# Moving three operands of a seven-product projection ahead of its last producer, and splitting the other four at its end

## The chip, the cores and the metric

The kernel runs on one core of a Trainium2 chip. The metric is device time in microseconds (us) of one execution. Five engines matter: TensorE (PE) multiplies, with its weight loads listed apart (PEld); VectorE (DVE), ScalarE (ACT) and GpSimd (POOL) do the element-wise work; SyncE (SP) issues nearly all DMAs. Each engine works through its own queue in order.

## The reference, cut to what matters

Two decoder layers on a sequence of 1024 with a model width of 1024. Each ends with an output projection, a residual add, an RMSNorm and a convolutional FFN:

```python
def conv_ffn(h, w_up, w_dw, b_dw, w_down):
    u = h @ w_up                                  # 1024 -> 2 * 2816
    u = causal_dwconv(u, w_dw, b_dw)              # width 3
    gate, val = jnp.split(u, 2, axis=-1)
    return (jax.nn.silu(gate) * val) @ w_down

x = x + jnp.concatenate([mix, mem_o], axis=-1) @ w_out[l]
x = x + conv_ffn(rmsnorm(x, g_ffn[l]), w_up[l], w_dw_f[l], b_dw_f[l], w_down[l])
```

Everything is float32 and has to come out with float32 accuracy.

## The kernel before

**Layout.** The residual stream lies transposed in eight tiles `x[0]` to `x[7]` of 128 channels by 1024 tokens; the halves of the sequence are `h0` and `h1` (512 tokens each). A float32 product is made of three matmuls: each operand is split into a rounded high half (a cast on ACT) and the remainder as a low half (a subtraction on DVE or POOL), and high by high, high by low and low by high are added (`split`, L76; `split_gain`, L162, which also applies the norm's gain).

**The up projection** is `h @ w_up` of both FFNs. It is cut into 2 by 2 blocks: the weights of one chunk of 128 gate and 128 value channels into A11, A12 (gate, first and second half of the model width) and A21, A22 (value); the stream into B11 = x[0..3] at h0, B12 at h1, B21 = x[4..7] at h0 and B22 at h1. Instead of eight block products it uses seven, with sums S1 to S4 of the A blocks (on POOL, `sums`, L452) and T1 to T4 of the B blocks (on DVE, `ffn_operands`, L362: L401 makes T1, L405 T2, L407 T3, L409 T4, in place in the tiles of x):

- p1 = A11 B11 and p2 = A12 B21 add up in PSUM bank X,
- p5 = S1 T1 and p3 = S4 B22 in bank V,
- p6 = S2 T2, p7 = S3 T3 and p4 = A22 T4 in bank Y,

and between the products of a bank DVE reads the bank (into `fuv` and `fug`, the two result halves). One product is a chain of 12 matmuls (four tiles k by three matmuls, `chain`, L336, matmuls at L345) of 128x128 weights and 512 columns. There are 22 chunks; the operands of B and T are made once for all of them and stay in SBUF, 56 tiles of 128x512: 24 under the tag `h2` in a pool of their own (`up0`, `up1`, opened by `ffn_begin` before the output projection) and 32 under the tag `h`, which until then hold the output projection's own inputs (`mxh`, `mxl`). Before the change T1, T2 and T3 are the ones in `h2`, and B11, B21, B22 and T4 go into `h`.

**The entry into the FFN.** The output projection adds its results to x tile by tile (`out_part`, L328, the add at L334); the last tile is x[7] both times. `ffn_operands` follows for k = 0 to 3: squares of x[k] and x[k+4] for the norm (ACT, summed by POOL at L396), stores of both to DRAM (SP, L390), then for this k the split or sum of all seven operands. The first two chunks are worked together, as p1, p5, p2, p3, then the norm's statistics (`rstd_rows`, eight tiny matmuls L133 and a row broadcast L123 for each half of the sequence), then p6, p7, p4. From chunk 2 on the loop is p1, p4 of the chunk before, p6, p5, p2, p7, p3.

**What sets the order.** A scheduler orders each engine's queue from the program's order as priority and its own idea of time; a buffer that is reused makes its new writer wait for the last reader of the old tile. The queues below were read from the built programs.

Of the kernel before, what the change touches and what calls it, by code (L numbers as in the profile page):

```python
# [51 lines left out]
class Trunk:  # L52
# [308 lines left out]
    def ffn_operands(self, l):  # L361

        nc = self.nc
        K2 = KD // 2
        gain = f"g_ffn{l}"
        x = self.x
        h0, h1 = slice(0, HS), slice(HS, S)  # L370
        names = ("B11", "B21", "B22", "T1", "T2", "T3", "T4")
        ops = {n: ([None] * K2, [None] * K2) for n in names}
        for n in names:
            for k in range(K2):
                for i in range(2):
                    if n in ("T1", "T2", "T3"):
                        t = self.fp.tile([P, HS], F32R, tag="h2", name=f"f{n}{i}{k}", bufs=6 * K2)
                    else:
                        t = self.htile(f"f{n}{i}{k}")
                    ops[n][i][k] = t  # L380

        def op(n, k):
            return ops[n][0][k], ops[n][1][k]

        acc = self.main.tile([P, S], F32, tag="rb", name="sacc")
        v = nc.vector
        for k in range(K2):
            for q in (k, k + K2):
                for sl in (h0, h1):
                    nc.sync.dma_start(self.d_x[:, q, sl], x[q][:, sl])  # L390
                    if q == 0:
                        nc.scalar.activation(acc[:, sl], x[q][:, sl], AF.Square)
                    else:
                        sq = self.nt("sq")
                        nc.scalar.activation(sq, x[q][:, sl], AF.Square)
                        nc.gpsimd.tensor_tensor(acc[:, sl], acc[:, sl], sq, op=ALU.add)  # L396
            g, g2 = self.vec(gain, k), self.vec(gain, k + K2)
            x11, x12, x21, x22 = x[k][:, h0], x[k][:, h1], x[k + K2][:, h0], x[k + K2][:, h1]
            self.split_gain(*op("B11", k), x11, g)
            nc.scalar.activation(x11, x11, AF.Copy, scale=g)  # L400
            v.scalar_tensor_tensor(x12, x12, g, x11, op0=ALU.mult, op1=ALU.subtract)  # L401
            self.split(*op("T1", k), x12, lo_eng=v)
            self.split_gain(*op("B21", k), x21, g2)
            self.split_gain(*op("B22", k), x22, g2)
            v.scalar_tensor_tensor(x22, x22, g2, x12, op0=ALU.mult, op1=ALU.subtract)  # L405
            self.split(*op("T2", k), x22, lo_eng=v)
            v.tensor_tensor(x11, x22, x11, op=ALU.subtract)  # L407
            self.split(*op("T3", k), x11, lo_eng=v)
            v.scalar_tensor_tensor(x21, x21, g2, x22, op0=ALU.mult, op1=ALU.subtract)  # L409
            self.split(*op("T4", k), x21, lo_eng=v)  # L410
        return ops, acc

    def ffn(self, l):
        nc, tc = self.nc, self.tc
# [2 lines left out]
        def unit(nm):  # L417
            return self.main.tile([P, S], F32, tag="x", name=f"f{nm}")

        with self.fstack:  # L420
# [31 lines left out]
            def sums(c):  # L452

                a, b = raws[c]
                s12 = unit("s12").rearrange("p (k c) -> p k c", k=KD)
                s4 = self.nt("s4").rearrange("p (k c) -> p k c", k=K2)
                g = nc.gpsimd
                g.tensor_tensor(s12[:, lo4], b[:, lo4], b[:, hi4], op=ALU.add)
                g.tensor_tensor(s12[:, hi4], s12[:, lo4], a[:, lo4], op=ALU.subtract)
                g.tensor_tensor(b[:, lo4], a[:, lo4], b[:, lo4], op=ALU.subtract)  # L460
                g.tensor_tensor(s4, a[:, hi4], s12[:, hi4], op=ALU.subtract)
                st[c] = {"A": {"S1": s12[:, lo4], "S2": s12[:, hi4], "S3": b[:, lo4], "S4": s4,
                               "A11": a[:, lo4], "A12": a[:, hi4], "A22": b[:, hi4]}}

# [3 lines left out]

            load(0)
            load(1)
            ops, acc = self.ffn_operands(l)
            sums(0)
            sums(1)
            ybanks = self.ps.tile([P, 2, HS], F32, tag="b2b", name="uY")
            rb = self.main.tile([P, S], F32, tag="rb", name="rb")
            h0, h1 = slice(0, HS), slice(HS, S)
# [16 lines left out]
            def p1(c):  # L495
                d = st[c]
                d["v"] = unit("uv")
                d["g"] = unit("ug")
                d, X = p(c, 1, "A11", "B11", "X", True)
                nc.scalar.copy(d["v"][:, h0], X)  # L500

            def p6(c):
                d, Y = p(c, 6, "S2", "T2", "Y", True)
                nc.vector.tensor_tensor(d["g"][:, h1], Y, d["v"][:, h0], op=ALU.add)
# [4 lines left out]

            def p2(c):  # L510
                d, X = p(c, 2, "A12", "B21", "X", False)
                if c < 2:
                    return
                nc.vector.tensor_tensor(d["g"][:, h0], X, rb[:, h0], op=ALU.mult)
                if c + 1 < NF:
                    sums(c + 1)
                    load(c + 2)

            def late2(c):
# [8 lines left out]
            def p3(c):  # L528
                d, V = p(c, 3, "S4", "B22", "V", False)
                if c > 1:  # L530
                    late3(c)

            def late3(c):
# [30 lines left out]
                return y  # L564


            for f in (p1, p5, p2, p3):
                f(0)
                f(1)
                if f == p2:  # L570
                    rstd_rows()
                    late2(0)
                    late2(1)
            p6(0)
            late3(0)
            p6(1)
            late3(1)
            load(2)
            sums(2)
            load(3)  # L580
            p7(0)
            p7(1)
            p4(0)
            for c in range(2, NF):
                for f, i in ((p1, 0), (p4, -1), (p6, 0), (p5, 0), (p2, 0), (p7, 0), (p3, 0)):
# [92 lines left out]
    def layer_a(self):  # L678
# [270 lines left out]
                self.split(*mx(hf, CT + ct), outs[ct][:, hf * HS:(hf + 1) * HS])  # L949

        wm = [self.load_wm(0, u) for u in range(2)]
        for k in range(KD):
            self.x[k] = self.main.tile([P, S], F32, tag="x", name=f"x1{k}")
            nc.sync.dma_start(self.x[k], self.xT[:, k])

# [46 lines left out]
    def layer_b(self):  # L1002
# [298 lines left out]
            nc.sync.dma_start(self.x[k], self.d_x[:, k])  # L1301

        def out_loads():
            wos[0] = self.load_wo(1, 0)
            for k in (6, 7, 0):
                load_mix(k)
            for k in range(EARLY):
                load_x(k)
            for k in (1, 2, 3):
                load_mix(k)  # L1310
            for m in range(1, EARLY):
                wos[m] = self.load_wo(1, m)

        def out_steps():
            ks = [6, 7, 0, 1, 2, 3]
            d = {}

            def step(m, hf, j):
                k = ks[j]
                sl = slice(hf * HS, (hf + 1) * HS)  # L1320
                wh, wl = wos[m]
                if j == 0:
                    d["u"] = self.ps.tile([P, HS], F32, tag="c0", name="op")
# [3 lines left out]
            return [lambda m=m, hf=hf, j=j: step(m, hf, j) for m in range(EARLY) for hf in range(2)  # L1327
                    for j in range(len(ks))]

        for n, (t, e, I) in enumerate(its):  # L1330
# [21 lines left out]
        self.drain_fill()  # L1352
        stack.close()
        self.ffn_begin(1)
        ms = [m for m in (2, 4, 5, 6, 3, 7)]
        self.ps.n = 0
        for k in ms:
            load_x(k)
# [1 line left out]
        for m in ms:  # L1360
            w = self.load_wo(1, m)
            for hf in range(2):
                self.out_part(m, hf, w, mxh, mxl, order)
            if m == EARLY:
                for m0 in range(EARLY):
                    for hf in range(2):
                        self.out_part(m0, hf, wos[m0], mxh, mxl, order[-2:])

    NRAW = 2
    EARLY = 2  # L1370
    OLOAD = 40
    OFILL = 40
    VMARKS = (1.1, 1.0, 1.1, 0.7, 0)
# [163 lines left out]
```

## Time and profile before

| what | value |
|---|---|
| time, median of 3 runs (lowest, highest) | 2375.9 us (2375.04, 2375.92) |
| the profiled execution's own time, and its span | 2374.32 us, 2372.5 us |
| mean granted clock of TensorE | 0.981 |
| PE busy (share of the span), instructions | 2269.8 us (96%), 10970 |
| DVE busy | 1457.4 us (61%), 1967 |
| ACT busy | 1075.7 us (45%), 1864 |
| POOL busy | 1374.7 us (58%), 1031 |

The span runs from the first to the last instruction. A granted clock of 1.00 is 2.4 GHz, 0.50 is 1.2 GHz. The matmuls of the first FFN's up projection begin at 425.14 us and those of the second's at 1651.16 us; the stretch that begins at each of these points is called the first and the second entry.

### The profile page before, as it was taken

The numbers are of one execution on the slowest core, as the hardware profiler recorded it, in microseconds if no ns is written. First come the engines' busy times: TensorE is split into PE (matmuls) and PEld (weight loads), VectorE is DVE, ScalarE is ACT, GpSimd is POOL, SyncE is SP. The second block draws the span as 40 slices with busy tenths as digits, with TensorE's granted clock in tenths as the row PEclk, the third lists the DMA queues.
The fourth block names the chain that finished last, engine by engine and source line by source line (L and its number), as shares of the span: only waits on it lengthen the run. The fifth ranks groups of instructions, "written<-read, shape, count | busy, mean of one in ns | idle before, by whom it ended". The sixth has DMA issues, their size and how long they took to land.

```text
span 2372.5 us, 29724 instructions
## 1 busy us (share of the span) xinstructions
PE 2269.8 (96%) x10970; PEld 1872.0 (79%) x10970; DVE 1457.4 (61%) x1967; ACT 1075.7 (45%) x1864; POOL 1374.7 (58%) x1031
## 2 busy tenths in 40 slices
PE   6999889899999999999998999999799999999998
PEld 6777678677878887888897888777577787888887
DVE  7479775866666653225646777854766666655225
ACT  6786654533434343223543656844433443443212
POOL 3685946676777765553324444526576868676532
PEclk8999989999999999999999999999899999999999
DMA  6101113122222235333322222342122222235322
GB/s 238 36 27 36 47 45 126 50 89 72 80 80 89 80 112 188 100 107 116 116 86 76 79 74 75 109 148 85 36 89 80 89 71 90 71 129 176 113 71 72
DMA packets 85281, 216.74 MB, mean 91 GB/s; under 512 B 9008, under 2 KB 29232, under 8 KB 85136
## 3 DMA queue, kind: packets, MB, share of 16 engines
q1 hardware_dynamic: 84992, 214.52, 28.2%
q8 instruction: 86, 1.41, 0.2%
q14 instruction: 59, 0.48, 0.1%
q10 hardware_dynamic: 144, 0.32, 0.0%
HBM read 156.94 MB, written 51.58 MB: 88 GB/s over the span
## 4 chain that ended last, share of the span: by engine, by line
PE 44%; DVE 4%; issue 1%; ACT 1%; POOL 1%; DMA 0%; DVEq 0%; ACTq 0%; POOLq 0%; SPq 0%
PE uY L345 7%; PE uV L345 5%; PE uX L345 5%; PE dn L109 3%; PE dn L108 3%; PE dn L110 3%; PE vps L1079 3%; PE pq L108 2%; PE pq L110 2%; PE pq L109 2%; PE op L109 1%; PE op L108 1%; PE fo L1262 1%; PE fo L1261 1%; PE op L110 1%
## 5 line engine op out<-in xcount | busy, mean ns | idle before, releaser
L345 PE MATMUL uY<-fT,fwh 128*128 128x512 f32 x1056 | 333.0, 396 | 9.6 <-DVE fuv L525 6.6
L109 PE MATMUL dn<-gl,wd_hi 128*128 128x512 f32 (+1 forms) x752 | 284.6, 379 | 0.4 <-POOL gl L82 0.4
L108 PE MATMUL dn<-gh,wd_hi 128*128 128x512 f32 (+1 forms) x752 | 280.8, 378 | 1.3 <-ACT fx L618 1.3
L110 PE MATMUL dn<-gh,wd_lo 128*128 128x512 f32 (+1 forms) x752 | 279.1, 375 | 0.0
L619 DVE TENSOR_TENSOR fx<-fx,dn 128x512 f32<-128x512 f32 (+1 forms) x176 | 111.0, 637 | 270.9 <-PE dn L110 269.4
L345 PEld LDWEIGHTS uY<-fT,fwh 128*128 128x128 f32 x1056 | 197.0, 188 | 61.6 <-DVE fuv L525 13.4
L345 PE MATMUL uX<-fB,fwh 128*128 128x512 f32 x704 | 224.1, 398 | 16.8 <-ACT fB L168 7.3
L345 PE MATMUL uY<-fT,fwl 128*128 128x512 f32 x528 | 207.9, 394 | 0.0
L82 POOL TENSOR_TENSOR fwl<-wa,fwh 128x512 fp32r<-128x512 f32 x88 | 118.5, 1347 | 120.1 <-ACT fwh L81 116.6
L82 POOL TENSOR_TENSOR wd_lo<-wd_raw,wd_hi 128x1024 fp32r<-128x1024 f32 x44 | 107.7, 2454 | 128.1 <-ACT wd_hi L81 128.1
L345 PEld LDWEIGHTS uX<-fB,fwh 128*128 128x128 f32 x704 | 132.8, 190 | 50.4 <-ACT fB L168 7.7
L108 PEld LDWEIGHTS dn<-gh,wd_hi 128*128 128x128 f32 x752 | 141.1, 188 | 30.0 <-ACT fx L618 1.7
L110 PEld LDWEIGHTS dn<-gh,wd_lo 128*128 128x128 f32 x752 | 141.1, 188 | 27.2
L109 PEld LDWEIGHTS dn<-gl,wd_hi 128*128 128x128 f32 x752 | 141.3, 188 | 25.8 <-POOL gl L82 0.9
L82 POOL TENSOR_TENSOR fwl<-wb,fwh 128x512 fp32r<-128x512 f32 x88 | 117.2, 1335 | 72.7 <-ACT fwh L81 72.7
L832 POOL TENSOR_TENSOR yp<-yp,ct 128x512 f32<-128x512 f32 x100 | 135.6, 1359 | 27.5 <-ACT ct L831 22.5
L82 POOL TENSOR_TENSOR gl<-g,gh 128x512 fp32r<-128x512 f32 x88 | 116.8, 1348 | 55.1 <-ACT gh L81 55.1
L82 POOL TENSOR_TENSOR fwl<-fs,fwh 128x512 fp32r<-128x512 f32 x88 | 117.9, 1341 | 47.3 <-ACT fwh L81 47.3
L345 PE MATMUL uX<-fB,fwl 128*128 128x512 f32 x352 | 137.8, 394 | 0.0
L81 ACT CAST fwh<-wa 128x512 fp32r<-128x512 f32 x88 | 54.3, 619 | 149.1 <-PE uY L345 105.5
L345 PE MATMUL uV<-fT,fwh 128*128 128x512 f32 x352 | 113.7, 403 | 5.1 <-ACT fT L81 4.3
L345 PEld LDWEIGHTS uY<-fT,fwl 128*128 128x128 f32 x528 | 99.4, 188 | 23.3
(392 smaller groups left out, 6269.9 us busy)
## 6 DMA issues: line engine op xcount, KB each, us to landing
wb<-in_wup SPq DMA_DIRECT2D x44, 512.0 KB
wa<-in_wup SPq DMA_DIRECT2D x44, 512.0 KB
d_g<-fsg SPq DMA_DIRECT2D x44, 512.0 KB
wd_raw<-in_wdn SPq DMA_DIRECT2D x44, 512.0 KB
g<-d_g SPq DMA_DIRECT2D x44, 512.0 KB
d_x<-x SPq DMA_DIRECT2D x32, 256.0 KB
nxs<-d_x SPq DMA_DIRECT2D x32, 256.0 KB
wia_raw<-in_wia SPq DMA_DIRECT2D x14, 512.0 KB
```

What stands on the lines that cost most here:

```text
L81: nc.scalar.copy(hi, src)
L82: (lo_eng or nc.gpsimd).tensor_tensor(lo, src, hi.bitcast(F32), op=ALU.subtract)
L108: nc.tensor.matmul(out, lhsT=ah, rhs=bh, start=start and i == 0, stop=False)
L109: nc.tensor.matmul(out, lhsT=ah, rhs=bl, start=False, stop=False)
L110: nc.tensor.matmul(out, lhsT=al, rhs=bh, start=False, stop=stop and i == n - 1)
L345: mm = nc.tensor.matmul(out, lhsT=w[:, k], rhs=h[k], start=start and k == 0 and j == 0, stop=k == n - 1 and j == 2, skip_group_check=True)
L619: return nc.vector.tensor_tensor(self.x[m][:, sl], self.x[m][:, sl], ps, op=ALU.add)
L832: nc.gpsimd.tensor_tensor(y[:, hf], y[:, hf], c, op=ALU.add)
L1079: nc.tensor.matmul(ps, lhsT=a[hf][k][:, tsl], rhs=w[:, k % 4], start=k == 0 and j == 0, stop=k == KD - 1 and j == 2)
L1261: nc.tensor.matmul(po, lhsT=vs[:, j], rhs=ph[:, u], start=j == 0, stop=False)
L1262: nc.tensor.matmul(po, lhsT=vs[:, j], rhs=pl[:, u], start=False, stop=j == 2 * I + 1)
```

## The change

It changes which operands are made when. B11, T1 and B22 now live in `h2`, the pool that is open during the output projection, and are split there as soon as their tile of x is complete. B21 stays unsplit in x[4..7], and T2, T3 and T4 are kept as plain sums in the tiles of x (T2 over B22, T3 over B11, T4 over T1). They are split into `h` tiles by the new function `late`, called after p1 of the first two chunks. The sum S1 of these two chunks gets small tiles of its own (`sum1`); S2 and S4 share a unit that waits for a tile of x. The order of the products of the first two chunks becomes p1, p5, p3, p2, p6, p7, p4, with the norm's statistics after p6 in the program. In the first layer x[4..7] are loaded ahead of x[0..3]; in the second the output projection works on x[4], x[5] early and x[6], 0, 1, 2, 3, 7 after it, where it was 0, 1 early and then 2, 4, 5, 6, 3, 7. No operation is added or dropped; both programs make the same splits, sums, adds and matmuls.

```diff
-        names = ("B11", "B21", "B22", "T1", "T2", "T3", "T4")
+        names = ("B11", "T1", "B22", "B21", "T2", "T3", "T4")
         ops = {n: ([None] * K2, [None] * K2) for n in names}
-        for n in names:
+        for n in names[:3]:
             for k in range(K2):
                 for i in range(2):
-                    if n in ("T1", "T2", "T3"):
-                        t = self.fp.tile([P, HS], F32R, tag="h2", name=f"f{n}{i}{k}", bufs=6 * K2)
-                    else:
-                        t = self.htile(f"f{n}{i}{k}")
-                    ops[n][i][k] = t
+                    ops[n][i][k] = self.fp.tile([P, HS], F32R, tag="h2", name=f"f{n}{i}{k}", bufs=6 * K2)
...
-            self.split_gain(*op("B11", k), x11, g)
             nc.scalar.activation(x11, x11, AF.Copy, scale=g)
+            self.split(*op("B11", k), x11, lo_eng=v)
             v.scalar_tensor_tensor(x12, x12, g, x11, op0=ALU.mult, op1=ALU.subtract)
             self.split(*op("T1", k), x12, lo_eng=v)
-            self.split_gain(*op("B21", k), x21, g2)
             self.split_gain(*op("B22", k), x22, g2)
             v.scalar_tensor_tensor(x22, x22, g2, x12, op0=ALU.mult, op1=ALU.subtract)
-            self.split(*op("T2", k), x22, lo_eng=v)
             v.tensor_tensor(x11, x22, x11, op=ALU.subtract)
-            self.split(*op("T3", k), x11, lo_eng=v)
-            v.scalar_tensor_tensor(x21, x21, g2, x22, op0=ALU.mult, op1=ALU.subtract)
-            self.split(*op("T4", k), x21, lo_eng=v)
-        return ops, acc
+            v.scalar_tensor_tensor(x12, x21, g2, x22, op0=ALU.mult, op1=ALU.subtract)
+        def late():
+            for k in range(K2):
+                for n, sl, q in (("B21", h0, k + K2), ("T2", h1, k + K2)):
+                    for i in range(2):
+                        ops[n][i][k] = self.htile(f"f{n}{i}{k}")
+                    self.split_gain(*op(n, k), x[q][:, sl], self.vec(gain, q) if n == "B21" else None)
+            for k in range(K2):
+                for n, sl in (("T3", h0), ("T4", h1)):
+                    for i in range(2):
+                        ops[n][i][k] = self.htile(f"f{n}{i}{k}")
+                    self.split(*op(n, k), x[k][:, sl], lo_eng=v)
+        return ops, acc, late
...
             def sums(c):
                 a, b = raws[c]
-                s12 = unit("s12").rearrange("p (k c) -> p k c", k=KD)
-                s4 = self.nt("s4").rearrange("p (k c) -> p k c", k=K2)
+                if c < 2:
+                    s1 = first[c]
+                    u = unit("s24").rearrange("p (k c) -> p k c", k=KD)
+                    s2, s4 = u[:, lo4], u[:, hi4]
+                else:
...
+            def sum1(c):
+                s1 = first[c] = self.nt("s1").rearrange("p (k c) -> p k c", k=K2)
+                b = raws[c][1]
+                nc.gpsimd.tensor_tensor(s1, b[:, lo4], b[:, hi4], op=ALU.add)
...
-            ops, acc = self.ffn_operands(l)
-            sums(0)
-            sums(1)
+            ops, acc, late = self.ffn_operands(l)
...
-            for f in (p1, p5, p2, p3):
-                f(0)
-                f(1)
-                if f == p2:
+            for c in range(2):
+                begin(c)
+                sum1(c)
+            p1(0)
+            p1(1)
+            late()
+            for c in range(2):
+                sums(c)
+            for c in range(2):
+                st[c]["g"] = unit("ug")
+            for f in (p5, p3, p2, p6, p7):
+                for c in range(2):
+                    f(c)
+                if f == p6:
                     rstd_rows()
-                    late2(0)
-                    late2(1)
-            p6(0)
-            late3(0)
-            p6(1)
-            late3(1)
-            load(2)
-            sums(2)
-            load(3)
-            p7(0)
-            p7(1)
+                    for c in range(2):
+                        out2(c)
+                        out3(c)
+                if f == p6:
+                    load(2)
+                    begin(2)
+                    sums(2)
+                    load(3)
             p4(0)
...
-        for k in range(KD):
+        for k in (4, 5, 6, 7, 0, 1, 2, 3):
             self.x[k] = self.main.tile([P, S], F32, tag="x", name=f"x1{k}")
...
-        ms = [m for m in (2, 4, 5, 6, 3, 7)]
+        ms = (6, 0, 1, 2, 3, 7)
...
-    EARLY = 2
+    EARLY = (4, 5)
```

How the change moves instructions is seen at two places, both at the second entry.

DVE there, before. In the names `fT113` is the low half (1) of T1 for tile 3, `x27` is x[7] of the second layer, `L508` is the first add that reads bank V after p5. The last operands of k = 2, then of k = 3:

```order
L82 TENSOR_TENSOR fT112_14373<-x22_13948,fT102_14372 128x512
L82 TENSOR_TENSOR fT212_14381<-x26_13954,fT202_14380 128x512
L82 TENSOR_TENSOR fT312_14389<-x22_13948,fT302_14388 128x512
L82 TENSOR_TENSOR fT412_14397<-x26_13954,fT402_14396 128x512
L169 SCALAR_TENSOR_TENSOR fB1113_14351<-x23_13956,vecs_63,fB1103_14350 128x512
L169 SCALAR_TENSOR_TENSOR fB2113_14359<-x27_13958,vecs_63,fB2103_14358 128x512
L142 RECIPROCAL rs_14668<-sd_14666 128x4
L169 SCALAR_TENSOR_TENSOR fB2213_14367<-x27_13958,vecs_63,fB2203_14366 128x512
L401 SCALAR_TENSOR_TENSOR x23_13956<-x23_13956,vecs_63 128x512
L405 SCALAR_TENSOR_TENSOR x27_13958<-x27_13958,vecs_63,x23_13956 128x512
L82 TENSOR_TENSOR fT113_14375<-x23_13956,fT103_14374 128x512
L407 TENSOR_TENSOR x23_13956<-x27_13958,x23_13956 128x512
```

DVE at the same place, now; the last output tile's add, B22 for k = 3 (`fB2213`), the three sums and T2's low half for k = 3 stand directly ahead of these rows, and `L530` is the same add as `L508`:

```order
L82 TENSOR_TENSOR fT310_14548<-x20_13950,fT300_14547 128x512
L82 TENSOR_TENSOR fT410_14552<-x20_13950,fT400_14551 128x512
L142 RECIPROCAL rs_14722<-sd_14720 128x4
L82 TENSOR_TENSOR fT311_14556<-x21_13952,fT301_14555 128x512
L82 TENSOR_TENSOR fT411_14560<-x21_13952,fT401_14559 128x512
L142 RECIPROCAL rs_14730<-sd_14728 128x4
L82 TENSOR_TENSOR fT312_14564<-x22_13954,fT302_14563 128x512
L82 TENSOR_TENSOR fT412_14568<-x22_13954,fT402_14567 128x512
L82 TENSOR_TENSOR fT313_14572<-x23_13956,fT303_14571 128x512
L530 TENSOR_TENSOR fuv_14479<-uV_14589,fuv_14479 128x512
L82 TENSOR_TENSOR fT413_14576<-x23_13956,fT403_14575 128x512
L530 TENSOR_TENSOR fuv_14498<-uV_14607,fuv_14498 128x512
```

T1's low half for k = 3 (`fT113`) stood seven rows behind T4's for k = 2 (`fT412`) and behind the splits of `x27`; now it stands ahead of the last tile's add. T3 and T4, whose splits stood with their own k, now follow all together, ahead of the adds that read bank V.

POOL there, before, from the last square but one (`sacc`) on, `fs12` being the unit with S1 and S2, `wb` with S3, `ns4` with S4:

```order
L396 TENSOR_TENSOR sacc_14400<-sacc_14400,nsq_14511 128x512
L458 TENSOR_TENSOR fs12_14537<-wb_13944 128x512
L458 TENSOR_TENSOR fs12_14543<-wb_13946 128x512
L459 TENSOR_TENSOR fs12_14537<-fs12_14537,wa_14340 128x512
L460 TENSOR_TENSOR wb_13944<-wa_14340,wb_13944 128x512
L459 TENSOR_TENSOR fs12_14543<-fs12_14543,wa_14342 128x512
L460 TENSOR_TENSOR wb_13946<-wa_14342,wb_13946 128x512
L82 TENSOR_TENSOR fwl_14591<-fs12_14537,fwh_14590 128x512
L82 TENSOR_TENSOR fwl_14624<-wa_14340,fwh_14623 128x512
L461 TENSOR_TENSOR ns4_14538<-wa_14340,fs12_14537 128x512
```

POOL there, now, `ns1` being S1 and `fs24` the unit with S2 and S4:

```order
L392 TENSOR_TENSOR sacc_14368<-sacc_14368,nsq_14455 128x512
L484 TENSOR_TENSOR ns1_14475<-wb_13944 128x512
L484 TENSOR_TENSOR ns1_14477<-wb_13946 128x512
L392 TENSOR_TENSOR sacc_14368<-sacc_14368,nsq_14459 128x512
L473 TENSOR_TENSOR wb_13944<-wa_14340,wb_13944 128x512
L82 TENSOR_TENSOR fwl_14591<-ns1_14475,fwh_14590 128x512
L473 TENSOR_TENSOR wb_13946<-wa_14342,wb_13946 128x512
L82 TENSOR_TENSOR fwl_14591<-ns1_14477,fwh_14590 128x512
L471 TENSOR_TENSOR fs24_14579<-ns1_14475,wa_14340 128x512
L471 TENSOR_TENSOR fs24_14583<-ns1_14477,wa_14342 128x512
L472 TENSOR_TENSOR fs24_14579<-wa_14340,fs24_14579 128x512
L82 TENSOR_TENSOR fwl2_14684<-fs24_14579,fwh2_14683 128x512
```

S1 of both chunks now comes first, and the last square's sum goes ahead of S3; the rest follows without a gap in the queue's order, S2 and S4 last.

## Rows read from the trace of the kernel before

**Rows 1.** Windows view, second output projection: busy us of each engine, then clock, DMA.
```profile
core 0: us, PE busy (x) PEld busy (x) DVE busy (x) ACT busy (x) POOL busy (x), PEclk, DMA share, GB/s
1600.00:1640.00 40.00, 40.00 (x178) 33.14 (x177) 4.81 (x7) 10.56 (x16) 23.86 (x17) 1.00 0.34 117
```

**Rows 2.** Timeline of PE at both entries: start, us, engine, line, operation.
```profile
425.14 0.63 PE L345 MATMUL uV<-fT,fwh 128*128 128x512 f32 x2
...
1651.16 0.62 PE L345 MATMUL uX<-fB,fwh 128*128 128x512 f32 x2
...
1652.54 0.95 PE L133 MATMUL st<-ones,sacc 128*128 128x1 f32 x8
1653.35 0.95 PE L345 MATMUL uX<-fB,fwh 128*128 128x512 f32 x3
```

**Rows 3.** Waits of PE, 425 to 462 us: us in total, times, longest.
```profile
PE uX L345 <- DVE x L334: 3.4, 1, 3.4
PE st L133 <- ACT sd L140: 1.2, 1, 1.2
PE uV L345 <- ACT fT L81: 0.7, 1, 0.7
PE st L133 <- POOL sacc L396: 0.7, 1, 0.7
```

**Rows 4.** Waits of PE, 462 to 505 us.
```profile
PE uY L345 <- DVE fuv L525: 1.8, 1, 1.8
PE uY L345 <- DVE fug L504: 0.9, 1, 0.9
```

**Rows 5.** Waits of PE, 1651 to 1692 us.
```profile
PE uX L345 <- ACT fB L168: 7.3, 1, 7.3
PE uX L345 <- DVE fB L169: 3.7, 1, 3.7
PE uV L345 <- ACT fT L81: 3.6, 1, 3.6
PE uV L345 <- ACT fwh L81: 0.8, 1, 0.8
```

**Rows 6.** Waits of PE, 1692 to 1745 us.
```profile
PE uY L345 <- DVE fuv L525: 2.2, 2, 1.9
PE uY L345 <- DVE fug L504: 2.1, 2, 1.3
```

**Rows 7.** Windows view, the stretches of matmuls at half clock after the waits.
```profile
434.60:438.60 4.00, 3.91 (x10) 3.10 (x11) 4.00 (x5) 3.40 (x6) 2.89 (x2) 0.53 0.77 234
442.20:445.20 3.00, 2.92 (x8) 2.31 (x9) 3.00 (x6) 2.25 (x6) 0.00 (x0) 0.51 0.00 0
...
1664.20:1667.00 2.80, 2.75 (x6) 1.82 (x6) 2.80 (x2) 1.22 (x2) 2.80 (x3) 0.50 0.00 0
1670.80:1673.00 2.20, 2.08 (x4) 1.17 (x4) 2.20 (x2) 1.23 (x2) 2.20 (x2) 0.50 0.00 0
1676.50:1684.70 8.20, 8.19 (x29) 7.03 (x29) 8.13 (x13) 5.63 (x10) 1.63 (x1) 0.53 0.01 6
1714.70:1718.50 3.80, 3.80 (x12) 2.94 (x11) 1.04 (x2) 2.62 (x5) 1.17 (x1) 0.55 0.02 4
```

**Rows 8.** Timeline of DVE, second entry.
```profile
1653.88 0.68 DVE L334 TENSOR_TENSOR x<-x,op 128x512 f32<-128x512 f32 x1
...
1662.41 6.71 DVE L82 TENSOR_TENSOR fT<-x,fT 128x512 fp32r<-128x512 f32 x4
...
1677.90 2.49 DVE L82 TENSOR_TENSOR fT<-x,fT 128x512 fp32r<-128x512 f32 x4
```

**Rows 9.** Timeline of POOL: with DVE nearly idle, and beside DVE's splits.
```profile
1612.05 5.08 POOL L396 TENSOR_TENSOR sacc<-sacc,nsq 128x512 f32<-128x512 f32 x4
...
1666.86 1.71 POOL L82 TENSOR_TENSOR fwl<-wa,fwh 128x512 fp32r<-128x512 f32 x1
```

**Rows 10.** Timeline of ACT: a high half with gain, and the last square.
```profile
1640.94 0.73 ACT L168 ACTIVATE fB<-x,vecs 128x512 fp32r<-128x512 f32 x1 [4.42 <-PE op L109]
...
1655.02 0.63 ACT L395 ACTIVATE nsq<-x 128x512 f32<-128x512 f32 x1
```

More of the change, by code (lines that the diff above doesn't have):

```diff
@@ L454, in sums, with begin @@
                 a, b = raws[c]
-                s12 = unit("s12").rearrange("p (k c) -> p k c", k=KD)
-                s4 = self.nt("s4").rearrange("p (k c) -> p k c", k=K2)
+                if c < 2:
[3 more added lines that the diff above has]
+                else:
+                    u = unit("s12").rearrange("p (k c) -> p k c", k=KD)
+                    s1, s2 = u[:, lo4], u[:, hi4]
+                    s4 = self.nt("s4").rearrange("p (k c) -> p k c", k=K2)
                 g = nc.gpsimd
-                g.tensor_tensor(s12[:, lo4], b[:, lo4], b[:, hi4], op=ALU.add)
-                g.tensor_tensor(s12[:, hi4], s12[:, lo4], a[:, lo4], op=ALU.subtract)
+                if c > 1:
+                    g.tensor_tensor(s1, b[:, lo4], b[:, hi4], op=ALU.add)
+                g.tensor_tensor(s2, s1, a[:, lo4], op=ALU.subtract)
+                g.tensor_tensor(s4, a[:, hi4], s2, op=ALU.subtract)
                 g.tensor_tensor(b[:, lo4], a[:, lo4], b[:, lo4], op=ALU.subtract)
-                g.tensor_tensor(s4, a[:, hi4], s12[:, hi4], op=ALU.subtract)
-                st[c] = {"A": {"S1": s12[:, lo4], "S2": s12[:, hi4], "S3": b[:, lo4], "S4": s4,
-                               "A11": a[:, lo4], "A12": a[:, hi4], "A22": b[:, hi4]}}
+                st[c]["A"].update({"S1": s1, "S2": s2, "S3": b[:, lo4], "S4": s4,
+                                   "A12": a[:, hi4], "A22": b[:, hi4]})
+            def begin(c):
+                st[c] = {"A": {"A11": raws[c][0][:, lo4]}}
+            def sum1(c):
+                s1 = first[c] = self.nt("s1").rearrange("p (k c) -> p k c", k=K2)
+                b = raws[c][1]
+                nc.gpsimd.tensor_tensor(s1, b[:, lo4], b[:, hi4], op=ALU.add)
+            first = {}
             load(0)
             load(1)
-            ops, acc = self.ffn_operands(l)
-            sums(0)
-            sums(1)
+            ops, acc, late = self.ffn_operands(l)
             ybanks = self.ps.tile([P, 2, HS], F32, tag="b2b", name="uY")
@@ L497, in p1 @@
                 d["v"] = unit("uv")
-                d["g"] = unit("ug")
+                if c > 1:
+                    d["g"] = unit("ug")
                 d, X = p(c, 1, "A11", "B11", "X", True)
@@ L511, in p2, with out2 @@
                 d, X = p(c, 2, "A12", "B21", "X", False)
[L512 to L515, printed above, removed]
+                if c > 1:
+                    out2(c)
+                if 1 < c < NF - 1:
+                    begin(c + 1)
                     sums(c + 1)
                     load(c + 2)
-            def late2(c):
+            def out2(c):
                 d = st[c]
@@ L530, in p3, with out3 @@
                 if c > 1:
-                    late3(c)
-            def late3(c):
+                    out3(c)
+            def out3(c):
                 d = st[c]
@@ L564, in conv @@
                 return y
-            for f in (p1, p5, p2, p3):
-                f(0)
-                f(1)
-                if f == p2:
-                    rstd_rows()
-                    late2(0)
-                    late2(1)
-            p6(0)
-            late3(0)
-            p6(1)
-            late3(1)
-            load(2)
-            sums(2)
-            load(3)
-            p7(0)
-            p7(1)
+            for c in range(2):
[12 more added lines that the diff above has]
+                if f == p6:
+                    rstd_rows()
+                    for c in range(2):
+                        out2(c)
+                        out3(c)
+                if f == p6:
[3 more added lines that the diff above has]
+                    load(3)
             p4(0)
@@ L1303, in out_loads @@
         def out_loads():
-            wos[0] = self.load_wo(1, 0)
+            wos[EARLY[0]] = self.load_wo(1, EARLY[0])
             for k in (6, 7, 0):
                 load_mix(k)
-            for k in range(EARLY):
+            for k in EARLY:
                 load_x(k)
@@ L1310, in out_loads @@
                 load_mix(k)
-            for m in range(1, EARLY):
+            for m in EARLY[1:]:
                 wos[m] = self.load_wo(1, m)
@@ L1326, in step @@
                     nc.vector.tensor_tensor(self.x[m][:, sl], self.x[m][:, sl], d["u"], op=ALU.add)
-            return [lambda m=m, hf=hf, j=j: step(m, hf, j) for m in range(EARLY) for hf in range(2)
+            return [lambda m=m, hf=hf, j=j: step(m, hf, j) for m in EARLY for hf in range(2)
                     for j in range(len(ks))]
@@ L1363, in layer_b @@
                 self.out_part(m, hf, w, mxh, mxl, order)
-            if m == EARLY:
-                for m0 in range(EARLY):
+            if m == ms[0]:
+                for m0 in EARLY:
                     for hf in range(2):
```

## The prediction

> **What bounds the kernel now.** I read the windows view first, on the stretch that feeds the second up projection. TensorE is busy all of 40 us at full clock, with 178 matmuls, so one matmul costs 40/178 = 0.23 us; DVE has 4.81 us of work there, POOL 23.86 [rows 1]. Where matmuls run densely nothing on another engine can be felt. The timeline of PE gives the two points at which this ends, 425.14 and 1651.16 us, and the price of one group of the norm's statistic matmuls, 1653.35 - 1652.54 = 0.81 us [rows 2].
>
> The waits of PE behind these points show what is lost. First entry: 3.4 + 1.2 + 0.7 + 0.7 = 6.0 us for operands and statistics [rows 3], then 1.8 + 0.9 = 2.7 us in bank Y, where PE waits for DVE's reads [rows 4]. Second entry: 7.3 + 3.7 + 3.6 + 0.8 = 15.4 us, nearly all for high and low halves of B and T [rows 5], then 2.2 + 2.1 = 4.3 us [rows 6]. Behind each cluster of waits the windows view shows matmuls at a granted clock near 0.5, the 1.2 GHz level: 4.0 + 3.0 us in the first entry, 2.8 + 2.2 + 8.2 + 3.8 = 17.0 us in the second [rows 7]; half of that is lost, 3.5 and 8.5 us. Together the two entries lose 6.0 + 2.7 + 3.5 + 15.4 + 4.3 + 8.5 = 40.4 us, and only there can the change act.
>
> What ends last in them is DVE's queue. An operation of 512 columns takes it 0.62 us when POOL is idle (2.49/4) but 1.68 us beside POOL's sums (6.71/4) [rows 8]; POOL's take 1.27 us with DVE idle (5.08/4) and 1.71 beside those splits [rows 9]. So one pair of DVE and POOL operations costs both 1.68 us.
>
> **The change part by part.**
>
> *Early splits.* B11, T1 and B22 and the three sums of k = 0, 1, 2 move under the projection: seven DVE operations per k. The 40 us of [rows 1] hold 17 POOL operations; if each is paired with a DVE one, that is 17 x 1.68 = 28.6 us, the other four of 21 take 4 x 0.62 = 2.5, the seven adds 4.8: 35.9 of 40 us, so it fits, with little to spare. TensorE is dense there: cost nothing. If the cover goes, each operation still queued when the projection ends costs 1.68 us (rival 3).
>
> *What still has to follow the last matmul.* DVE's new order, from the end of the projection: the last add 0.68 [rows 8]; then it waits for ACT's square 0.63 and high half 0.73 [rows 10], 2.04 us together; then 12 operations with two SBUF inputs (B22's low half for k = 3, three sums, T2's low half, four of T3, three of T4), two reciprocals, and only then the add that reads bank V after p5, which lets the B22 product into V. POOL has S3, S1's splits, S2 and S4 of two chunks queued the whole time, so each of the 12 could cost 0.62 or 1.68 us; I take 1.68, since the row of four splits beside POOL's sums is this very place and kind of work. The end is 2.0 + 12 x 1.68 + 0.2 + 0.7 = 23.1 us after the last matmul; with 0.62 it would be 10.3.
>
> *What TensorE has meanwhile.* p1 and p5 of both chunks and two matmuls of p6: 50 x 0.23 = 11.5 us, and four statistic groups, 4 x 0.81 = 3.2: 14.7 us. All its operands are ready except the statistics' reciprocals. So it idles 23.1 - 14.7 = **8.4 us in each entry**: about 3.5 at the broadcast, which waits for a reciprocal behind seven of the 12, and 5 at the B22 product.
>
> *Afterwards.* S2, S3 and S4 come from POOL at one pair per 1.7 us and T3, T4 are complete by then, while the products spaced over 8 us each use them. Late waits between none and today's 2.7 and 4.3 us; I take 1 us per entry, nearer to none, because the operands that today are made last are now made first. Half clock between none and today's 3.5 and 8.5 us; I take 3 per entry, near the first entry's row, whose waits (6.0) are nearest to 8.4.
>
> *Costed at nothing.* The new order of x loads in the first layer: the loads go ahead of the convolutions and the scan, far from the first add that needs x; if one is late, an add waits and bank reuse stalls the projection. The stores of x keep their order on SP; but a sum in place now waits for its store. A store is half a tile, 256 KB; at the 117 GB/s of [rows 1] it takes 2.2 us (an estimate). For k up to 2 a tile of projection hides it; for x[7] it lands 0.7 + 2.2 = 2.9 us after the last matmul, where DVE comes to the sum at 2.0 + 1.7 = 3.7. Bounds 0 and 2 us. The relabelled tiles of the second projection are the same work in the same number. Separate tiles for S1 add no operation. Raw weight buffers of chunks 2 and 3 come free some microseconds later; their products are 168 matmuls away.
>
> *Sum.* First entry: (8.4 - 6.0) + (3 - 3.5) + (1 - 2.7) = +0.2 us. Second: (8.4 - 15.4) + (3 - 8.5) + (1 - 4.3) = -15.8. Together -15.6 against the profiled execution's 2374.3 us: 2358.7. The median of the runs stands 1.6 above that execution, so **2360 us**.
>
> **The rivals.**
>
> 1. *A pair of operations costs the sum of both.* Then 1.27 + 0.62 = 1.89 us instead of 1.68, 12 x 0.21 = 2.5 us more per entry: 2365. For it: POOL's sums here read two SBUF operands, as DVE's do, and some sums in the same stretch may be dearer than the splits. Against: both rows beside each other say 1.68 and 1.71 [rows 8, 9]. Chance 0.12. The Trainium skill, page "SBUF — State Buffer", section "Who interferes with whom", states this rule: DVE and GpSimd share one port pair as an exclusive lock that is held for the whole instruction, and the loser fully blocks. By that rule moving DVE work beside POOL's gains nothing over running one after the other; the trace shows a pair somewhat below the sum.
>
> 2. *No contention at the entry.* If POOL's work falls beside TensorE's instead, DVE takes 0.62 us, its queue ends at 10.3 us, before TensorE's 14.7, and neither wait nor half clock follows: 2360 - 2 x 8.4 - 2 x 3 = 2337. Against it is POOL's order, which has no gap there. Chance 0.05.
>
> 3. *Slower: the early splits are not done by the end of the projection.* They share DVE with the adds that free the projection's banks, and the high halves share ACT. If the seven operations of k = 2 are still queued at its end, each entry takes 7 x 1.68 = 11.8 us more: 2384. It decides from 15.6/2/1.68 = 4.6 operations per entry on. For it: only 4 us of 40 are to spare. Against: the pairs in that sum are a worst case. Chance 0.07.
>
> 4. *Slower: the clock stays at its lower level.* Of the 168 matmuls of the first two chunks 118 come after the wait. All at half clock lose 118 x 0.23 = 27 us instead of 3, per entry: 2408. Against: in [rows 7] no stretch outlasts 8.2 us. Chance 0.03.
>
> 5. *It doesn't do what it says.* The total of waits only changes its place: the products of T2, T3, T4 now wait as those of B21 and T4 did: 2375.9. Chance 0.07.
>
> **How the numbers follow.** The forecast keeps 0.66. Its own range: without half clock and late waits 2360 - 8 = 2352; if two of the 12 operations are free of POOL, 2 x 1.06 us per entry less again, about 2347; with today's 3.5, 8.5, 2.7 and 4.3 instead of 8, it is 2371. To hold 8 in 10 the range goes up to 2376, rival 5; left out are rivals 2, 3 and 4 (0.15) and a tail of the forecast. A change under 0.2% (4.75 us) is about what a measurement can't tell from none. Faster: the forecast and rival 1 but for a few hundredths, and rival 2: 0.79. Same: rival 5 and those hundredths: 0.11. Slower: rivals 3 and 4: 0.10.
>
> **What would show it right or wrong.** Right: at both entries the first 48 matmuls follow without waits for B11 and T1; PE waits some 3.5 us at the broadcast for the reciprocal and some 5 us in V for DVE; DVE's splits of T3 and T4 take 1.6 to 1.7 us each; the waits of 7.3, 3.7 and 3.6 us are gone; the first entry stays about as long, the second is 16 us shorter. Wrong: waits for high halves of B11 or T1 (the early splits came late), a wait of V for POOL's S4 rather than for DVE, DVE operations near 0.62 us in the entry, new gaps in the projection's matmuls, or clock rows near 0.5 that go on past 10 us.

## The result

| what | before | changed |
|---|---|---|
| time, median of 4 runs (lowest, highest) | 2375.5 us (2373.6, 2375.9) | 2363.0 us (2361.1, 2364.3) |
| the profiled execution's own time, and its span | 2374.3, 2372.5 us | 2361.1, 2359.3 us |
| mean granted clock of TensorE | 0.981 | 0.984 |
| busy us: PE, DVE, ACT, POOL | 2269.8, 1457.4, 1075.7, 1374.7 | 2262.8, 1472.1, 1075.9, 1380.4 |

The ratio is 0.9948, interval [0.9931, 0.9966]. Later runs scatter more, and beside one set of them the gain was smaller (after_r below). By the profiled executions of two kernels that were each run twice, the second entry repeats to 0.1 us and the first to about 2 us.

Stages, from PE's timeline (from the end of the output projection to the last up-projection matmul): first 454.4 us before, 455.5 now; second 468.1 before, 454.3 now. The first projection ends 0.7 us later than before, and 1.3 us are won between the two FFNs, from a cause that was not looked for. So of the 13.2 us by which the span is shorter, the second stage gives 13.8, and the small terms nearly cancel.

Waits of PE in the changed kernel, first entry, then what comes late there; they answer to [rows 3, 4]:

```profile
PE uV L345 <- DVE fuv L530: 4.4, 1, 4.4
PE st L123 <- ACT fwh L81: 2.7, 1, 2.7
PE uX L345 <- DVE x L334: 2.5, 1, 2.5
PE uV L345 <- POOL fwl L82: 0.2, 1, 0.2
...
PE uX L345 <- ACT fuv L522: 1.0, 1, 1.0
PE uY L345 <- DVE fug L526: 0.8, 1, 0.8
PE uY L345 <- DVE fuv L547: 0.3, 1, 0.3
```

The second entry, 1648 to 1690 us, answers to [rows 5]; its late waits are the same three lines as above, against [rows 6]:

```profile
PE st L133 <- ACT sd L140: 4.2, 1, 4.2
PE uV L345 <- DVE fuv L530: 3.0, 1, 3.0
PE uV L345 <- ACT fwh L81: 1.7, 2, 1.5
```

The waits for B11, B21 and T1 (7.3, 3.7, 3.6 us) are gone. In their place stand the statistics and the add that reads bank V. DVE's timeline, second entry, from the last splits ahead of the projection's last add to that add of bank V:

```profile
1655.77 1.33 DVE L169 SCALAR_TENSOR_TENSOR fB<-x,vecs,fB 128x512 fp32r<-128x512 f32 x1 [0.77 <-ACT fB L168]
1657.03 0.68 DVE L334 TENSOR_TENSOR x<-x,op 128x512 f32<-128x512 f32 x1
1659.08 0.94 DVE L169 SCALAR_TENSOR_TENSOR fB<-x,vecs,fB 128x512 fp32r<-128x512 f32 x1 [1.37 <-ACT fB L168]
1660.05 1.65 DVE L400 SCALAR_TENSOR_TENSOR x<-x,vecs,x 128x512 f32<-128x512 f32 x1
...
1666.66 3.45 DVE L82 TENSOR_TENSOR fT<-x,fT 128x512 fp32r<-128x512 f32 x2
1670.03 0.16 DVE L142 RECIPROCAL rs<-sd 128x4 f32<-128x4 f32 x1
...
1673.48 5.10 DVE L82 TENSOR_TENSOR fT<-x,fT 128x512 fp32r<-128x512 f32 x3
1678.51 0.68 DVE L530 TENSOR_TENSOR fuv<-uV,fuv 128x512 f32<-128x512 f32 x1
```

The projection ended at 1651.75. Its last add began 5.3 us later (2.7 before the change, [rows 8]). DVE was busy with earlier splits without a gap until 1655.00; then a low half of B21, ahead of the add in the queue, waited 0.77 us for its high half from ACT and took 1.33. From 1660.05 on DVE runs without a gap at 1.64 to 1.78 us per operation with two SBUF inputs, 1.66 from start to start. L530, with one operand in PSUM, takes 0.68 beside POOL.

Half clock, windows view, three stretches after the waits, answering to [rows 7]:

```profile
428.40:433.00 4.60, 4.51 (x14) 3.60 (x14) 2.56 (x4) 2.43 (x5) 3.70 (x3) 0.63 0.25 94
...
448.00:456.00 8.00, 3.58 (x14) 2.95 (x14) 6.92 (x6) 2.89 (x6) 8.00 (x6) 0.59 0.01 2
1665.60:1672.50 6.90, 6.90 (x27) 5.99 (x28) 6.90 (x6) 3.74 (x8) 6.90 (x5) 0.58 0.00 0
```

The second entry has 6.9 us of matmuls at 0.58 instead of 17.0 near 0.5.

### The profile page after: what moved, and what is told of

The parts are those of the page before. It is cut to its first block, busy times and chain, and to the rows that moved or that the text cites. A ratio compares the mean times of both kernels' runs of the same rounds, so it can differ in the third digit from the quotient of the medians.

```text
span 2359.3 us, 29756 instructions
## 1 busy us (share of the span) xinstructions
PE 2262.8 (96%) x10970; PEld 1868.8 (79%) x10970; DVE 1472.1 (62%) x1967; ACT 1075.9 (46%) x1864; POOL 1380.4 (59%) x1031
## 4 chain that ended last, share of the span: by engine, by line
PE 81%; DVE 10%; ACT 3%; issue 2%; POOL 2%; DMA 2%; DVEq 0%; ACTq 0%; POOLq 0%
PE uY L345 15%; PE uX L345 10%; PE uV L345 10%; PE dn L109 7%; PE dn L108 7%; PE dn L110 7%; PE vps L1108 3%; PE pq L108 2%; PE pq L110 2%; PE pq L109 2%; DVE fT L82 1%; PE fo L1291 1%; PE ft L1282 1%; PE fo L1290 1%; PE fs L1246 1%
## 5 line engine op out<-in xcount | busy, mean ns | idle before, releaser
L345 PE MATMUL uV<-fB,fwh 128*128 128x512 f32 x352 | 111.6, 395 | 7.4 <-DVE fuv L530 7.4
```

Source lines behind the costliest of these rows:

```text
L345: mm = nc.tensor.matmul(out, lhsT=w[:, k], rhs=h[k], start=start and k == 0 and j == 0, stop=k == n - 1 and j == 2, skip_group_check=True)
```

## The experiments

The theory after the result: the second entry gains because the operands of p1, p5 and p3 now stand ahead of the others in DVE's queue, which runs at POOL's pace. Rivals: the product order or the kept sums alone carry it; the early splits do; the queue is long for ACT's sake.

To compare entries without the scatter of whole runs, the table gives the time from the projection's end to the start of the 337th matmul of the up projection (first four chunks), counted in PE's timeline; without any loss it would be 336 x 0.23 = 77 us, and 3 more for the statistics. The ratios compare with runs of the kernel before that were taken beside each.

| kernel | first entry | second entry | ratio to before, interval |
|---|---|---|---|
| before | 95.6 | 110.3 | |
| changed; again, as after_r | 97.8; 99.5 | 96.5; 96.5 | 0.9948 [0.9931, 0.9966]; 0.9986 [0.9971, 1.0002] |
| pool_only | 98.0 | 96.1 | 0.9943 [0.9926, 0.9960] |
| pool_back | 101.2 | 97.8 | 0.9994 [0.9976, 1.0012] |
| keep_only | 98.5 | 101.6 | 0.9983 [0.9965, 1.0001] |
| order_back; again, as order_back_r | 92.6; 92.2 | 91.4; 91.4 | 0.9933 [0.9907, 0.9960]; 0.9926 [0.9905, 0.9948] |
| nosums | 87.4 | 90.0 | 0.9870 [0.9847, 0.9893] |
| x_back | 99.3 | 95.8 | 0.9946 [0.9931, 0.9961] |
| order_s1 | 93.5 | 96.3 | 0.9939 [0.9922, 0.9955] |
| order_p6_s1 | 96.3 | 94.2 | 0.9938 [0.9922, 0.9954] |
| best_early | 92.4 | 89.2 | 0.9936 [0.9909, 0.9962] |

**pool_only.**

```diff
-                    if n in ("T1", "T2", "T3"):
+                    if n in ("B11", "T1", "B22"):
```

(an edit of the kernel before)

> The kernel before with one edit: B11, T1 and B22 take the tiles of the pool that is open during the projection, T2, T3 and B21 the others; no kept sums, no new product order, no new load order. Theory (the gain comes from which operands can be split under the projection): the waits for high and low halves of B and T in the second entry (15.4 us) fall below 9 us, and the time comes to 2361 to 2367 us. Rival (the kept sums with their late splits and the product order carry the gain): within 3 us of 2375.5.

2364.7 us, inside the theory's range. One line gives the second entry what the whole change gives it (the first takes 98.0, as in the changed kernel). The waits there, 1648 to 1695 us:

```profile
PE uX L345 <- ACT fuv L500: 3.2, 1, 3.2
PE uX L345 <- DVE fB L169: 1.6, 1, 1.6
PE uV L345 <- DVE x L334: 1.2, 1, 1.2
```

They fall from 15.4 to 6.0 us, as the theory wanted.

**pool_back.**

```diff
-                    ops[n][i][k] = self.fp.tile([P, HS], F32R, tag="h2", name=f"f{n}{i}{k}", bufs=6 * K2)
+                    ops[n][i][k] = self.htile(f"f{n}{i}{k}")
```

(for B11, T1, B22; T2, T3 and T4 get the other tag in `late`, not shown)

> The changed kernel with the two groups of operands exchanged between the pools again: T2, T3, T4 where the pool is open early, B11, T1, B22 and B21 in the tiles that the projection's inputs hold; sums, late splits and product order stay as changed. Theory: B11 and T1 come late again, the second entry waits over 13 us, 2372 to 2382 us. Rival (order and kept sums carry the gain): 2361 to 2366 us.

2377.9 us (nine runs from 2370.7 to 2385.4, one of 7359.5), inside the theory's range, but not for its reason: the second entry takes 97.8, not 110, with waits of 9.8 us:

```profile
PE st L123 <- DVE rs L142: 3.5, 1, 3.5
PE uV L345 <- DVE fuv L531: 3.0, 1, 3.0
PE uV L345 <- ACT fwh L81: 2.4, 1, 2.4
PE st L133 <- POOL wb L474: 0.9, 1, 0.9
```

So the tiles of the early pool aren't needed there; being first in the queue is enough. It isn't a test of splits that all come after the projection: as its tiles came free, DVE began them at 1652.64, 9.6 us before the projection's end. The time went elsewhere, in the profiled execution: 3.4 us more than the changed kernel in the first entry, and far from the entries two long operations of DVE, behind each of which PE stood 5.3 us (last section).

**keep_only.** pool_back with the product order of before.

```diff
-            for f in (p5, p3, p2, p6, p7):
+            for f in (p5, p2, p3, p6, p7):
...
-                if f == p6:
+                if f == p2:
                     rstd_rows()
```

> The changed kernel with the pools exchanged back (B11, T1, B22 late) and the product order of before: of the change only the kept sums with their late splits are left. Theory now (what counts is that the operands of p1, p5 and p3 stand ahead of the others in DVE's queue; being made under the projection adds less): 336 matmuls take 94 to 98 us in each entry, against 95.6 and 110.3 before. Rival (early splits are needed as well): second entry over 102 us.

98.5 and 101.6 us (2369.5 in all): above the theory's range and just below the rival's. With both entries at the old product order: the pools alone change the second entry by 96.1 - 110.3 = -14.2 us, the kept sums (with the new tile order) by -8.7, both together (order_back) by -18.9. The parts overlap; in the first entry only both together win, 95.6 to 92.6. Against pool_back, the product order of before costs 3.8 us in the second entry (101.6 against 97.8) and gains 2.7 in the first.

**order_back.** The changed kernel with the last diff alone (the third adds of bank V, `out3`, stay after p6).

> The changed kernel with the product order of before in the first two chunks: p1, p5, p2, p3, statistics after p2, then p6, p7. Theory: the products wait for the same queue of DVE, in V or elsewhere, so the order is worth little: within 3 us of 2363. Rival (the product order is part of the gain): 3 to 8 us slower, 2366 to 2371, with waits for X or Y that the changed kernel doesn't show.

2358.6 us, better than either theory: 5.2 and 5.1 us less in the two entries. The rival had the sign reversed: with the early pool the new product order is a loss (with the late tiles it gained 3.8 us in the second entry, pool_back against keep_only). Its waits, 1648 to 1695 us:

```profile
PE uV L345 <- DVE fuv L530: 1.7, 1, 1.7
PE uY L345 <- DVE fuv L547: 1.4, 1, 1.4
PE uV L345 <- ACT fwh L81: 1.2, 1, 1.2
PE st L133 <- ACT sd L140: 1.0, 1, 1.0
PE uX L345 <- ACT fuv L522: 0.8, 1, 0.8
```

The V add begins 26.6 us after the projection's end as in the changed kernel (26.8), but PE has 74 matmuls ahead of the product that needs it, not 50, and p2's can start while the statistics are made.

**nosums.** Without POOL's S2, S3 and S4 of the first two chunks.

```diff
...
+                if c < 2:
+                    st[c]["A"].update({"S1": s1, "S2": s1, "S3": b[:, lo4], "S4": a[:, hi4],
+                                       "A12": a[:, hi4], "A22": b[:, hi4]})
+                    return
```

> The changed kernel without POOL's sums S2, S3 and S4 for the first two chunks of both FFNs (their products use A12, A21 and S1 unsummed): six sums per FFN less on POOL, everything else is kept. Theory (DVE's 12 operations at the entry run at POOL's pace): DVE's splits of T3, T4 fall from 1.7 to below 1.2 us on the mean, the add that PE waits for in V comes 5 us or more earlier, the wait in V (4.4 and 3.0 us) falls below 1 us; 2350 to 2357 us. Rival (DVE's queue is long for another reason, ACT's high halves): DVE's operations start as late as before, 2360 to 2363 us.

2347.2 us, below the theory's range, but not by the theory's step. The lines of T3's and T4's splits in the second entry, first the changed kernel (1658 to 1690 us; count, busy us, mean ns), then nosums (1650 to 1690):

```profile
L82 DVE TENSOR_TENSOR fT<-x,fT 128x512 fp32r<-128x512 f32 x8 | 13.1, 1671 | 0.0
```

```profile
L82 DVE TENSOR_TENSOR fT<-x,fT 128x512 fp32r<-128x512 f32 x8 | 9.8, 1278 | 0.0
```

DVE's timeline in nosums, second entry, around the add of bank V (`L532` here):

```profile
1656.06 1.76 DVE L166 TENSOR_TENSOR fT<-x,fT 128x512 fp32r<-128x512 f32 x1
...
1657.83 1.68 DVE L82 TENSOR_TENSOR fT<-x,fT 128x512 fp32r<-128x512 f32 x1
1659.44 0.68 DVE L532 TENSOR_TENSOR fuv<-uV,fuv 128x512 f32<-128x512 f32 x1
1660.04 6.30 DVE L82 TENSOR_TENSOR fT<-x,fT 128x512 fp32r<-128x512 f32 x4
...
1666.35 1.86 DVE L82 TENSOR_TENSOR fT<-x,fT 128x512 fp32r<-128x512 f32 x3
```

The mean missed the 1.2 us that was expected: while POOL has work the splits still take 1.6 us, and only the last three, with POOL done, 0.62. That difference shows whose pace DVE keeps. The gain is another matter: up to the V add the operations take as long as in the changed kernel (1.65 to 1.77 us). The add begins 16.1 us after the projection instead of 26.8 because it now stands behind one of the eight splits instead of seven, and six times 1.7 us is 10.2 of these 10.7 us. So the run doesn't show that the gain comes from a faster pace. An edit that moves this add alone, with POOL's sums kept, was not run.

**order_s1.** order_back, with S1 of both chunks made by a hook in `ffn_operands`.

```diff
             for q in (k, k + K2):
+                if q == KD - 1:
+                    hook()
...
```

> The changed kernel with the product order of before (p1, p5, p2, p3, p6, p7, p4 of the first two chunks) and S1 of both chunks issued before the squares of the last tile, not after them. 72 matmuls now stand ahead of the first B22 product in V, where the changed kernel has 50, and the statistics come after them. Theory (PE lacked work while DVE's and POOL's queue ran): the matmuls up to the 336th after the projection take 88 to 92 us in each entry (97.8 and 96.5 in the changed kernel, 92.6 and 91.4 with the product order alone); 2352 to 2359 us. Rival (POOL's last sums of squares now come behind S1's splits, and the statistics become the bound): waits of PE for the statistics of over 3 us in each entry, no better than the product order alone.

2358.6 us; the matmuls took 93.5 and 96.3: the second entry is 4.9 us worse than order_back's, the first within its scatter, and the stated rival is not the reason either. Waits, 1640 to 1695 us:

```profile
PE uV L345 <- DVE x L334: 4.0, 1, 4.0
PE uV L345 <- POOL fwl L82: 3.8, 2, 2.4
PE uV L345 <- ACT fwh L81: 0.4, 1, 0.4
```

POOL's work, moved under the end of the projection, slows DVE's splits there: the last add of the projection begins 11.6 us after its end, against 5.1 in order_back, and its PSUM bank is released as late. The four splits just ahead of that add take 1.74 to 1.79 us; in order_back 0.68 to 0.75, but for the last (1.34).

**order_p6_s1.** The same with p6 ahead of p3, `(p5, p2, p6, p3, p7)`.

> As order_s1 with p6 ahead of p3 in the program (p1, p5, p2, p6, p3, p7, p4). Theory: 84 matmuls ahead of the first B22 product; 336 matmuls take 87 to 91 us, 0 to 2 us less than order_s1. Rival (S2's low half from POOL and T2 of k = 3 are late, PE waits in Y instead): 1 to 4 us more than order_s1.

96.3 and 94.2 us, 2.8 more and 2.1 less than order_s1: neither theory, and no gain in time (2359.1 us).

**x_back.**

```diff
-        for k in (4, 5, 6, 7, 0, 1, 2, 3):
+        for k in range(KD):
...
-        ms = (6, 0, 1, 2, 3, 7)
+        ms = (2, 4, 5, 6, 3, 7)
...
-    EARLY = (4, 5)
+    EARLY = (0, 1)
```

> The changed kernel with the order of x loads in the first layer (0 to 7) and of the second output projection (0, 1 early, then 2, 4, 5, 6, 3, 7) as before. Theory: the load order costs the 0.7 us by which the first projection ends later; the second order decides which k is complete when, and k = 2 then stands close to the end: the second entry's 336 matmuls take 97 to 101 us (96.5 changed). Rival (neither matters): within 0.5 us in both entries, the first projection's end as late.

2361.6 us. Missed by both: the second entry is 0.7 us shorter, not longer, and the first 1.5 longer, within its scatter; the second projection's last add begins 3.0 us after its end, not 5.3. The first projection's end (425.2, changed 425.9 and 423.6 again) varies too much to be put down to the loads.

**after_r, order_back_r, best_early.** Side by side; best_early is order_back with `EARLY` and `ms` of x_back.

> The changed kernel as it is, beside the two that follow on the same chip: 2361 to 2365 us, both theories.

> The changed kernel with the product order of before, a second time, on the same chip as the changed kernel. Theory (the new product order leaves PE 50 matmuls ahead of the first B22 product in V, the old one 74, and costs 5 us in each entry by the matmuls' times): 2356 to 2360 us, 4 to 7 us below the changed kernel. Rival (what the entry saves, a later stretch gives back): within 2 us of the changed kernel.

> As order_back_r, with the order of tiles in the second output projection as before (0, 1 early, then 2, 4, 5, 6, 3, 7). Theory: the last add of the projection comes 2 us earlier in DVE's queue of the second entry (it began 5.3 us after the projection's end in the changed kernel and 3.0 with this order), so 0 to 2 us below order_back_r. Rival: no difference beyond 1 us, since PE's waits in V have shrunk already.

The changed kernel came to 2372.2 us here (2362.9 to 2386.5), order_back_r to 2356.6 (2351.7 to 2367.2), best_early to 2365.1 (2346.6 to 2372.3). By these times after_r and best_early missed both theories, and order_back_r, inside its theory's 2356 to 2360, lies 15.6 us below the changed kernel, not 4 to 7. The kernel before took 2375.05 us beside them (18 runs), so the whole change measured 2.9 us here, which is not clear of noise. Its profiled execution, the fastest of 12, has the entries of the first (99.5 and 96.5); what slowed the others was not profiled. In the entries the theories hold: 7.3 and 5.1 us for the product order, 2.2 more in the second for the tile order. Both lowest times lie below any of the changed kernel, 2361.1, but best_early's median isn't reliably better; the last section has a likely reason.

## Why the prediction was right

The time (2363.0 against 2360 forecast), its direction and its place came as forecast: 12.5 us of the 15.6. By the table the second entry gained 13.8 us (15.8 forecast) and the first lost 2.2 (0.2 forecast). The waits that were to go went, and DVE's chain is what PE waits for in V; but the closeness of the sum is in part luck, as one of its errors hides most of another (below), and after_r had only 2.9 us of the gain left in its median. How much of the queue's length is ACT's doing was not separated by a run.

- *The waits that go.* 7.3, 3.7 and 3.6 us went as said, and the two forecast waits in V and at the statistics came: 9.8 and 8.9 us of idle time in the entries against 8.4 each.
- *DVE's chain.* The pace was right: the first of the 12 operations took 0.94 us, the other 11 came every 1.66, against 1.68 forecast (rival 1 had 1.89), and the splits of 0.62 us in nosums, with POOL done, show that POOL sets it. From the last add's start to the end of L530 it took 22.2 us (23.1 forecast). Wrong was its start: the chain was begun at the last matmul, but the last add came 5.2 and 5.3 us later, behind a backlog of splits. L530 ended 27.4 us after the projection, not 23.1. This is the term that was mis-sized, by 4.3 us, a small form of rival 3. The B22 product began 27.6 us after the projection; up to there the second entry lost 27.6 - 14.7 = 12.9 us, where the sum had 8.4 + 3 = 11.4. Most of the 4.3 us is hidden by the second error: the half clock falls ahead of this wait and only fills it, while the sum added its 3 us to the 8.4.
- *The bank.* The late add also holds a PSUM bank: 2.5 us at the first entry's first matmul, which no term had, though 3.4 of the 6.0 us in [rows 3] are the same kind of wait.
- *The statistics.* In the first entry the wait came as forecast, 2.7 us against 3.5: the broadcast (L123) began when DVE's second reciprocal was done. The waits view names a cast on ACT that ended at the same moment.

```profile
447.53 0.17 DVE L142 RECIPROCAL rs<-sd 128x4 f32<-128x4 f32 x1
...
447.84 1.13 PE L123 MATMUL st<-ident,rs 128*128 128x128 f32 x8 [2.70 <-ACT fwh L81]
```

  In the second entry the 4.2 us are at another link. The second group of statistic matmuls began when ACT had taken the root (`sd`, L140) of the first group, whose matmuls had run at 1657.20. In ACT's queue this root stood behind T2's high half (L165), which waited for DVE's first sum, then behind three more operations and a table load of 1.28 us. So the link is ACT's queue, with 1.2 us of waiting for DVE in it. POOL's last sum of squares (1659.43, 1.72 us) was done 4 us earlier.

```profile
1657.20 0.95 PE L133 MATMUL st<-ones,sacc 128*128 128x1 f32 x8
...
1661.74 0.62 ACT L165 CAST fT<-x 128x512 fp32r<-128x512 f32 x1 [1.19 <-DVE x L400]
...
1663.90 1.28 ACT L140 ACT_TABLE_LOAD   x1
1665.19 0.26 ACT L140 ACTIVATE sd<-st,eps_rms 128x4 f32<-128x4 f32 x1
...
1665.60 1.84 PE L133 MATMUL st<-ones,sacc 128*128 128x1 f32 x8 [4.19 <-ACT sd L140]
```

- *Late waits.* 1.0 + 0.8 + 0.3 = 2.1 us per entry, forecast 1.
- *Half clock.* 6.9 x (1 - 0.58) = 2.9 us in the second entry, forecast 3.
- *Costed at nothing.* "Early splits" were not quite free: they are the backlog in front of the last add. The load order's cost stays open.

What the sum did not see is that the change holds a loss: it took the 50 matmuls ahead of V as given and didn't price the order they replaced. order_back gives 5 us per entry back. And the early pool, on which the working dwelt, gives the second entry's whole gain by itself (pool_only, 14.2 us); the kept sums by themselves give 8.7 of it (keep_only).

## What to carry to other kernels

When an in-order engine feeds a dense consumer, put first what is consumed first; here that could be done by where tiles live or by when work is issued, and doing both gained less than the sum. Count what the consumer can do until the slowest link arrives, and order its work so that this is the most: here 24 matmuls more ahead of a wait were worth 5 us with the early pool, and in the second entry not with the late tiles. Look also at where the add that ends the wait stands in its own queue: in nosums it came 10.7 us earlier, nearly all by its place. Work moved under another stage wasn't free here: in order_s1 POOL's sums under the projection put its last add 6.6 us later.

## What had not been expected

One operation of the steady loop, a product of two SBUF operands on DVE, takes 0.68 to 7.97 us. DVE in best_early, far behind the entry, where POOL has work without a gap:

```profile
1814.34 1.28 DVE L578 SCALAR_TENSOR_TENSOR y<-fug,vecs,y 128x1023 f32<-128x1023 f32 x1
1815.53 7.97 DVE L548 TENSOR_TENSOR fuv<-fuv,rb 128x512 f32<-128x512 f32 x1
1823.41 1.27 DVE L580 SCALAR_TENSOR_TENSOR y<-fug,vecs,y 128x1022 f32<-128x1022 f32 x1
```

POOL there, the first and last of the six that ran inside it:

```profile
1815.43 1.33 POOL L82 TENSOR_TENSOR fwl<-fs,fwh 128x512 fp32r<-128x512 f32 x1
...
1821.66 1.29 POOL L470 TENSOR_TENSOR fs<-wb 128x512 f32<-128x512 f32 x1
```

The same operation in order_back_r:

```profile
1818.32 1.77 DVE L548 TENSOR_TENSOR fuv<-fuv,rb 128x512 f32<-128x512 f32 x1
```

and POOL's that it came after:

```profile
1818.24 1.30 POOL L82 TENSOR_TENSOR fwl<-fs,fwh 128x512 fp32r<-128x512 f32 x1
```

There it took its turn after one POOL operation; in best_early POOL's kept their pace and it came after six. PE stood 5.8 us each time:

```profile
PE uY L345 <- DVE fuv L565: 11.5, 2, 5.8
```

In the profiled executions of best_early and order_back it happened twice each (7.97 us), in pool_back's twice (7.47 us), in the changed kernel's not at all; before's longest case was 3.6 us. The price can be read behind the entry, from the 337th to the last matmul of an up projection: 357.6 to 358.8 us in every profiled execution without such an operation, 365.4 and 365.8 with one (pool_back, both FFNs), 374.0 and 373.9 with two (order_back and best_early, second FFN), so some 8 us each. The profile of order_back took 2369.9 us, that of order_back_r, the same kernel with none, 2352.0. The steps between the other runs of order_back_r (2351.7, 2352.2, 2361.1, 2364.8, 2367.2) would fit one or two, and those of after_r too, but only profiled executions show it. The Trainium skill, page "SBUF — State Buffer", section "Who interferes with whom", says that issue order decides who blocks, not the operation's shape. That the shape doesn't decide, these rows bear out, with 1.77 and 7.97 us for the same one. The order of issue doesn't explain them by itself: both times POOL's operation had begun about 0.1 us before DVE's, and in best_early five more that began after it still went ahead. Why, stays open.
